# First square stage: sums of weight quadrants by VectorE additions from plain loads in place of accumulating DMAs, and the same for T3 of the FFN's down projection

## The chip, the cores and the metric

The kernel runs on one core of one Trainium2 chip. The metric is the device time of one execution in microseconds (us), lower is better. A core has TensorE (PE in the profile, with its weight loads as PEld), VectorE (DVE), ScalarE (ACT), GpSimd (POOL) and SyncE (SP, which here only issues DMAs). The engines run side by side, each works through its own queue in order, and they wait for one another by semaphores.

## The reference

One decoder block on 1024 tokens of width 1024 in float32: a mixer of two parallel branches, a cross-attention to 256 memory tokens, a SwiGLU FFN, each behind an RMSNorm and added to the residual stream, and a last RMSNorm.

```python
proj = n @ w_in                       # z, xBC, dt, q, k, v, r, a1, g_ssd, g_gla
y_ssd = ssd_mixer(z, xBC, dt_raw, ...)        # chunked scan, gated norm
y_gla = gla_mixer(q, k, v, r, a1, ...)        # gated linear attention, chunked
merged = sigmoid(g_ssd) * (y_ssd @ w_up_ssd) + sigmoid(g_gla) * (y_gla @ w_up_gla)
h = x + merged @ w_o
h = h + cross_attention(rmsnorm(h), rmsnorm(mem), w_xq, w_xkv, w_xo)
g, u = split(rmsnorm(h) @ w_ffn_in, 2)
h = h + (silu(g) * u) @ w_ffn_out
out = rmsnorm(h)
```

## The kernel before

**Arithmetic.** Activations stand transposed, features by tokens. Each float32 operand is split into a high and a low part of a faster matmul type: ACT copies the high part (`split`, L225), DVE subtracts to get the low part (the helper at L74 records all DVE and POOL operations). A product of two operands is then three matmuls, high by high, high by low and low by high, on tiles of 128 by 128 weights and 128 by 512 activations.

**Seven sub-products.** Each large matrix product is done by a Strassen scheme: both operands are cut in four quadrants, and seven sub-products on quadrants or on sums of quadrants replace eight. Their names are B11, T1, T2, B22, T3, B21, T4, in the order `LATE` where two halves of a unit or a whole square product are worked. For the weight quadrants `w(i, j)` of a square product, the left operands are:

- B11: `w(0,0)`; B21: `w(0,1)`; T4: `w(1,1)`
- T1: `w(1,0) + w(1,1)`
- T2: T1's sum `+ w(0,0)`
- B22: T2's sum `+ w(0,1)`
- T3: `w(0,0) + w(1,0)`

The right operands are quadrants of the activations `X` or sums and differences of them, formed in place by DVE.

**Square products.** `Product` (L1129) is one 1024 by 1024 product. The four of them in a row (`prods`: w_up_ssd, w_up_gla, w_o, w_xq) run in the loop at L1305, 14 steps each (7 sub-products by two halves `kk` of the contraction), 24 matmuls a step. `build` (L1153) prepares the operands of a step, `mm` (L1169) issues its matmuls and, behind the second half, the evacuation of four PSUM banks. `DEPTH = 2`: operands are built two steps ahead. `load` (L1145) fetches a weight quadrant by two plain DMAs of 512 KB on SP's queue.

**Sums by DMA.** `plus` (L230) is a DMA on GpSimd's queue that adds its source to what stands in its destination. `load("T1")` brings `w(1,0)` and lets two `plus` add `w(1,1)`. `build` issues the next `plus` as soon as a sum has been split: `w(0,0)` and `w(0,1)` onto T1's tile for T2 and B22, `w(1,0)` onto B11's tile for T3. So each tile is loaded, added to, split, added to again.

**The stage ahead.** The first product's B11 operands are prepared within the last unit of the gate projection, `group(gg[3:], B)` (L1291), whose seven steps are counted by `n`. There B11 and T1 of the weights and the four quadrants of X (from `ys_d`) are loaded and the first two `build`s stand. Raw weights of B11 and T1 take slots of the key `aux` (4 slots, also used by the gate units), B21 and T4, loaded at steps 5 and 7, take slots of `op` (14 slots). The 14 operands of the input projection (two tiles for each of seven names) occupy all of `op` until the last gate unit has used them.

**FFN-down.** The loop at L1601 runs over `todo`: 7 sub-products by 6 pieces of the contraction (two blocks of 256 rows each, the last piece one). `stream` (L1513) loads the raw tiles (`fr`: right part from `act_d`, left part from `w_ffn_out`) six pieces ahead and splits them three pieces ahead into `fs`. T1, T2 and B22 take their left parts from running sums (`rs`, made by `plus`). T3 is `w(0,0)` by a plain load and `w(1,0)` by `plus` on top. The evacuation of a sub-product (`fevac`, L1568) writes into `o`; `fpost` transposes finished quadrants on PE, two of them behind each piece of T3 and of T4.

**Order.** The framework compiles the whole program into one queue per engine: it takes instructions in order of priority (program order, shifted by `high_priority` blocks such as `ahead()`), passes over what isn't ready by its own timing model, and hands out pool slots as they come free. So SP's order is not quite the order of the source lines.

Of the kernel before, what the change touches and what calls it, by code (L numbers as in the profile page):

```python
# [16 lines left out]
P = 128  # L17
# [3 lines left out]
HALF = TOK // 2  # L21
# [6 lines left out]
KP = D_FF // 256  # L28
# [51 lines left out]
def block_kernel(ctx: ExitStack, tc: tile.TileContext, t: dict, out: bass.AP):  # L80
# [147 lines left out]
    def plus(dst, src):  # L228

        nc.gpsimd.dma_start(out=dst, in_=src, accum_op=ALU.add)  # L230
# [4 lines left out]
    class Operands:  # L235
# [14 lines left out]
        def __init__(s, hb, kh, first=None, key="op", swap=0, last_key=None, order=None):  # L250
            s.B, s.kh, s.key, s.done, s.swap = {}, kh, key, 0, swap
            s.order = order or tuple(s.PLAN)
            s.last_key = last_key or key
            s.steps = s.build(hb, kh, first or (lambda *a: None))
# [874 lines left out]
    class Product:  # L1129
# [4 lines left out]
                 "B22": ((1, 1), None), "T3": ((0, 1), (sub, (1, 1), (0, 1))), "B21": ((1, 0), None),  # L1134
                 "T4": ((1, 0), (sub, (0, 0), (1, 0)))}

        def __init__(s, W, X, c, first, last, before=lambda n, late: None):
            s.W, s.X, s.first, s.last, s.before = W, X, first, last, before
            s.tags = (acc, bank) if c == 0 else (bank, acc)
            s.raw, s.hl = {}, {}  # L1140

# [3 lines left out]
        def load(s, name, key="op"):  # L1145
            r = s.raw[name] = slot(key, (P, 2, 2, HALF), name="raw")
            for kk in range(2):
                SP.dma_start(r[:, kk], s.w(*s.RAW[name], kk))
            if name == "T1":
                for kk in range(2):  # L1150
                    plus(r[:, kk], s.w(1, 1, kk))

        def build(s, t):  # L1153
            n, kk = divmod(t, 2)
            name = LATE[n]
            of, comb = s.RIGHT[name]
            q = lambda ij: s.X.quadrant(*ij)[:, 2 * kk:2 * kk + 2]
            x = [slot("op", (P, 2, 2, HALF), F32R, name="lr") for _ in range(2)]
            raw = s.raw[{"T2": "T1", "B22": "T1", "T3": "B11"}.get(name, name)][:, kk]
            split(raw, x[0][:, 0], x[0][:, 1], either(raw))  # L1160
            more = {"B11": (1, 0), "T1": (0, 0), "T2": (0, 1)}.get(name)
            if more:
                plus(raw, s.w(*more, kk))
            if comb:
                comb[0](either(raw, 1.0), q(of), q(comb[1]), q(comb[2]))
            split(q(of), x[1][:, 0], x[1][:, 1], either(raw), name == "T2")
            s.hl[t] = x
# [113 lines left out]
    def pre_xq(n, late):  # L1281
        if n == 5 and not late:
# [1 line left out]
            s1.close(1)  # L1284
            DVE.tensor_scalar(xsc, s1.r, XSC, None, ALU.mult)

    prods = [Product(t["w_up_ssd"], x_ys, 1, copied(y_ys), last_ys, pre_ys),
             Product(t["w_up_gla"], x_yg, 0, copied(x_wo), last_yg, pre_yg),
             Product(t["w_o"], x_wo, 1, *residual(r_wo, x_xq, h1_d, s1, "norm_xattn"), pre_wo),
             Product(t["w_xq"], x_xq, 0, copied(x_o), last_xq, pre_xq)]  # L1290
    for n, _ in enumerate(group(gg[3:], B)):  # L1291
        if n == 0:
            prods[0].load("B11", "aux")
            prods[0].load("T1", "aux")
        if n < 2:
            x_ys.load(ys_d, 0, n)
        elif n < 4:
            prods[0].build(n - 2)
        elif n < 6:
            x_ys.load(ys_d, 1, 5 - n)  # L1300
    settle_all()
    sums["m"] = pool("sa2", 2, stack=st5)

# [1 line left out]
    for t_ in range(4 * 14):  # L1305
        st, n = divmod(t_, 14)
        nxt, m = divmod(t_ + DEPTH, 14)
        if nxt < 4:
            prods[nxt].build(m)
        if n in (5, 7):  # L1310
            prods[st].load("B21" if n == 5 else "T4")
        elif n in (8, 9) and st < 3:
            prods[st + 1].load("B11" if n == 8 else "T1")
        if st == 0 and 6 <= n < 10:
            x_yg.load(yg_d, *((0, 0), (0, 1), (1, 1), (1, 0))[n - 6])
        prods[st].mm(n)

    kv = {}
# [177 lines left out]
    fq = lambda u, i, j: f_o[u][:, i, half(j)]  # L1496
    LEFT = {"B11": (0, 0), "B21": (0, 1), "T3": (0, 0), "T4": (1, 1)}
    todo = [(n, k, min(2, KP - k)) for n in range(7) for k in range(0, KP, 2)]
    raws, ops, run_sums = [], [], {}

    def w_out(i, j, k, kn):
        return t["w_ffn_out"][256 * k:256 * (k + kn), half(i)].rearrange("(k j p) c -> j p k c", j=2, p=P)[j]
# [10 lines left out]
    def stream(n_raw, n_ops):  # L1513

        while len(raws) < min(n_raw, len(todo)):
            n, k, kn = todo[len(raws)]
            name = LATE[n]
            r = slot("op", (P, 2, 2, HALF), name="fr")[:, :, :kn]
            SP.dma_start(r[:, 1], act_d[(n * KP + k) * P:(n * KP + k + kn) * P, :].rearrange("(k p) s -> p k s", p=P))
            if name in LEFT:  # L1520
                SP.dma_start(r[:, 0], w_out(*LEFT[name], k, kn))
            if name == "T3":
                plus(r[:, 0], w_out(1, 0, k, kn))
            raws.append(r)
        while len(ops) < min(n_ops, len(todo)):
            n, k, kn = todo[len(ops)]
            keys = ("op", ("aux", "aux", "m", "m", "op", "op")[k // 2]) if n == 6 else ("op", "op")
            x = [slot(key, (P, 2, 2, HALF), F32R, name="fs")[:, :, :kn] for key in keys]
            r, name = raws[len(ops)], LATE[n]
            with ahead():  # L1530
                split(r[:, 0] if name in LEFT else run_sums[k], x[0][:, 0], x[0][:, 1])
                if name in ("T1", "T2"):
                    plus(run_sums[k], w_out(0, LATE.index(name) - 1, k, kn))
                split(r[:, 1], x[1][:, 0], x[1][:, 1], neg=name == "T2")
            ops.append(x)
# [132 lines left out]
```

## Time and profile before

| | |
|---|---|
| median of 3 runs | 1966.55 us (1963.18 to 1967.26) |
| the profiled execution | 1970.81 us, of which the span of the profile is 1969.1 us |
| mean granted TensorE clock | 0.983 |
| 8 accumulating DMAs of w_up_ssd, first and last issue | 812.4 and 866.5 us |
| 6 accumulating DMAs of T3 in FFN-down, first and last issue | 1837.1 and 1871.2 us |

Times in the profile count from the start of the span. In a timeline a row has the start, the time from the first start to the last end, engine, line, operation, output and inputs, and the count of instructions merged; a bracket at its end is the idle time of the engine before it and what ended it. Matmuls overlap by pipelining, so single durations are longer than the spacing of their starts. A queue (`SPq`) row is the issue of a DMA, not its transfer. A window row has the length, then the busy time and number of instructions of PE, PEld, DVE, ACT and POOL, then the granted clock, the busy share of the DMA engines and GB/s.

### The profile page before, as it was taken

To read this page: it belongs to the slowest core of one execution; us is meant where nothing else is said; L and a number is where in the kernel's file an instruction comes from. 1 tells how busy PE (TensorE), PEld (TensorE's weight loads), DVE (VectorE), ACT (ScalarE), POOL (GpSimd) and SP (SyncE) were. 2 spreads that over 40 slices of the span, in tenths; PEclk is the share of its full clock that TensorE was granted. 3 is DMA by queue.
4 is the path that set the end of the run, shared out by engine and by line. 5 is a ranking of instruction groups with operands and counts; after the bars stand their busy time and mean duration, and the time that the engine had idled before them with its cause. 6 is when DMAs were issued, how large, how long until landed. Compare 5 with 4: busy or idle time off the path is not lost.

```text
span 1969.1 us, 25777 instructions
## 1 busy us (share of the span) xinstructions
PE 1886.7 (96%) x9500; PEld 1578.4 (80%) x9500; DVE 1388.8 (71%) x2128; ACT 990.3 (50%) x1674; POOL 258.4 (13%) x235
## 2 busy tenths in 40 slices
PE   7899999999999999979989999989999999999998
PEld 6898788877788888758868887868888888888788
DVE  5866668778786665448788787797677777764474
ACT  7535556565554554354536656564333433443352
POOL 1001100164553000011110010010000000001100
PEclk9999999999999999989999999989999999999999
DMA  8532434467566563877676723622233234498962
GB/s 276 177 119 73 156 128 171 145 200 219 174 193 198 162 189 124 260 183 178 151 201 186 179 65 52 194 97 80 86 125 111 80 107 134 116 316 220 240 209 86
DMA packets 242611, 313.23 MB, mean 159 GB/s; under 512 B 14747, under 2 KB 150149, under 8 KB 242485
## 3 DMA queue, kind: packets, MB, share of 16 engines
q1 hardware_dynamic: 225588, 279.08, 42.4%
q0 software_dynamic: 16896, 32.51, 10.3%
q8 instruction: 74, 1.21, 0.3%
q14 instruction: 53, 0.43, 0.1%
HBM read 226.28 MB, written 85.26 MB: 158 GB/s over the span
## 4 chain that ended last, share of the span: by engine, by line
PE 62%; issue 15%; DMA 9%; DVE 5%; ACT 4%; POOL 3%; SPq 1%; POOLq 0%; ACTq 0%; DVEq 0%
PE acc L52 49%; PE bank L52 12%; DVE X L74 1%; PE bank L56 1%; POOL raw L230 1%; DMA csb<-cs_d 1%; DMA rs<-in_w_ffn_out_dram 1%; DVE lr L74 1%; DMA fr<-in_w_ffn_out_dram 1%; ACT lr L225 1%; DVE wlo L74 1%; DMA raw<-in_w_up_gla_dram 1%; ACT e L874 1%; POOL rs L230 1%; DMA xT_d<-xs 0%
## 5 line engine op out<-in xcount | busy, mean ns | idle before, releaser
L225 ACT ACTIVATE whi<-raw 128x512 fp32r<-128x512 f32 x224 | 140.3, 630 | 174.1 <-PE acc L52 156.2
L52 PE MATMUL acc<-lr 128*128 128x512 f32 x864 | 205.2, 395 | 16.7 <-ACT o L368 6.2
L52 PEld LDWEIGHTS acc<-lr 128*128 128x128 f32 x864 | 163.3, 190 | 53.6 <-ACT o L368 6.6
L52 PE MATMUL bank<-lr 128*128 128x512 f32 x816 | 197.2, 401 | 8.7 <-ACT lr L225 3.1
L74 DVE TENSOR_TENSOR wlo<-raw,whi 128x512 fp32r<-128x512 f32 x224 | 157.5, 706 | 66.0 <-ACT whi L225 65.9
L52 PEld LDWEIGHTS bank<-lr 128*128 128x128 f32 x816 | 157.8, 194 | 45.0 <-ACT lr L225 3.5
L225 ACT ACTIVATE whi<-sa 128x512 fp32r<-128x512 f32 x144 | 90.7, 630 | 164.5 <-PE acc L52 114.7
L74 DVE TENSOR_TENSOR o<-acc,o 128x512 f32<-128x512 f32 x144 | 99.0, 688 | 71.8 <-PE acc L52 71.5
L74 DVE TENSOR_TENSOR lr<-raw,lr 128x1024 fp32r<-128x1024 f32 x70 | 85.4, 1220 | 91.1 <-ACT lr L225 91.1
L74 DVE TENSOR_TENSOR wlo<-sa,whi 128x512 fp32r<-128x512 f32 x144 | 105.3, 732 | 50.3 <-ACT whi L225 49.2
L225 ACT ACTIVATE lr<-raw 128x1024 fp32r<-128x1024 f32 x70 | 73.9, 1055 | 111.7 <-DMA raw<-in_w_up_ssd_dram 41.4
L52 PE MATMUL acc<-fs 128*128 128x512 f32 (+1 forms) x660 | 125.3, 349 | 0.0
L52 PEld LDWEIGHTS acc<-fs 128*128 128x128 f32 x660 | 107.1, 190 | 15.6
L74 DVE TENSOR_TENSOR fs<-fr,fs 128x1024 fp32r<-128x1024 f32 (+1 forms) x60 | 66.2, 1131 | 40.0 <-ACT fs L225 40.0
L52 PE MATMUL bank<-fs 128*128 128x512 f32 x396 | 90.2, 389 | 0.0
L52 PEld LDWEIGHTS bank<-fs 128*128 128x128 f32 x396 | 74.3, 188 | 15.4
L225 ACT ACTIVATE fs<-fr 128x1024 fp32r<-128x1024 f32 (+1 forms) x60 | 57.1, 981 | 58.9 <-DMA fr<-in_w_ffn_out_dram 28.2
L230 POOL DMA_DIRECT2D rs<-in_w_ffn_out_dram x18 | 21.1, 1254 | 474.9 <-DVE wlo L74 371.0
L52 PE MATMUL acc<-T1h,whi 128*128 128x512 f32 x192 | 76.6, 399 | 3.2 <-ACT whi L225 3.2
L52 PE MATMUL acc<-B22h,wlo 128*128 128x512 f32 x192 | 75.3, 392 | 3.6 <-DVE wlo L74 3.6
L52 PE MATMUL acc<-B11h,whi 128*128 128x512 f32 x192 | 76.1, 396 | 2.5 <-ACT whi L225 2.5
L52 PE MATMUL acc<-T2h,wlo 128*128 128x512 f32 x192 | 75.4, 393 | 2.9 <-DVE wlo L74 2.9
(395 smaller groups left out, 4961.8 us busy)
## 6 DMA issues: line engine op xcount, KB each, us to landing
raw<-in_w_in_dram SPq DMA_DIRECT2D x26, 1024.0 KB, 6.1
raw<-in_w_ffn_in_dram SPq DMA_DIRECT2D x22, 1024.0 KB, 8.3
act_d<-o SPq DMA_DIRECT2D x77, 256.0 KB, 2.3
fr<-act_d SPq DMA_DIRECT2D x35, 512.0 KB, 5.2
fr<-in_w_ffn_out_dram SPq DMA_DIRECT2D x20, 512.0 KB, 5.8
raw<-in_w_xkv_dram SPq DMA_DIRECT2D x8, 1024.0 KB, 10.8
csb<-cs_d SPq DMA_DIRECT2D x16, 512.0 KB, 4.9
h_d<-ga SPq DMA_DIRECT2D x32, 256.0 KB, 2.1
```

The source lines that it names most:

```text
L52: return s.e.matmul(o, x, y, **kw)
L56: return s.e.transpose(o, x, i)
L74: return f(*a, **kw)
L225: ACT.activation(hi, src, AF.Copy)
L230: nc.gpsimd.dma_start(out=dst, in_=src, accum_op=ALU.add)
L874: ACT.activation(s.e[:, h], s.csb[:, h], AF.Relu, bias=cs[:, s.i0 + h:s.i0 + h + 1], scale=-1.0)
```

## The change

In the first square product (`plain=True`) there are no accumulating DMAs. B11, T1's `w(1,0)`, T4's `w(1,1)` and B21's `w(0,1)` are fetched by plain loads, all four within the last gate unit, between the loads of X. A new tile S in an `op` slot holds the running sum, and DVE adds into it: `w(1,0) + w(1,1)` for T1, `+ w(0,0)` for T2, `+ w(0,1)` for B22; for T3, B11's tile is added onto T1's. `build(1)` goes from step 3 to step 6 of the gate unit, `build(0)` from 2 to 4. The loads of B21 and T4 at steps 5 and 7 of the product stay for the other three products. The loads of the second product's X (`x_yg`), at steps 6, 7, 8, 9 before, come at 6, 7, 9, 10.

In FFN-down, T3's second addend `w(1,0)` is fetched by three plain loads (of four, four and three blocks) into slots of the key `m`, and DVE adds it to the raw tile ahead of the split.

```diff
+        def left(s, name, kk):
+            r = lambda x: s.raw[x][:, kk]
+            if not s.plain:
+                return r({"T2": "T1", "B22": "T1", "T3": "B11"}.get(name, name))
+            if name == "T3":
+                add(DVE, r("T1"), r("T1"), r("B11"))
+                return r("T1")
+            if name in ("T1", "T2", "B22"):
+                if "S" not in s.raw:
+                    s.raw["S"] = slot("op", (P, 2, 2, HALF), name="raw")
+                x, y = {"T1": ("T1", "T4"), "T2": ("S", "B11"), "B22": ("S", "B21")}[name]
+                add(DVE, r("S"), r(x), r(y))
+                return r("S")
+            return r(name)
...
-            raw = s.raw[{"T2": "T1", "B22": "T1", "T3": "B11"}.get(name, name)][:, kk]
+            raw = s.left(name, kk)
             split(raw, x[0][:, 0], x[0][:, 1], either(raw))
...
-            if more:
+            if more and not s.plain:
                 plus(raw, s.w(*more, kk))
...
         if n == 0:
+            x_ys.load(ys_d, 0, 0)
             prods[0].load("B11", "aux")
+        elif n == 1:
             prods[0].load("T1", "aux")
-        if n < 2:
-            x_ys.load(ys_d, 0, n)
-        elif n < 4:
-            prods[0].build(n - 2)
-        elif n < 6:
-            x_ys.load(ys_d, 1, 5 - n)
+            prods[0].load("T4")
+        elif n == 2:
+            x_ys.load(ys_d, 0, 1)
+        elif n == 3:
+            x_ys.load(ys_d, 1, 1)
+        elif n == 4:
+            prods[0].load("B21")
+            prods[0].build(0)
+        elif n == 5:
+            x_ys.load(ys_d, 1, 0)
+        else:
+            prods[0].build(1)
...
-        if n in (5, 7):
+        if n in (5, 7) and st:
             prods[st].load("B21" if n == 5 else "T4")
...
-        if st == 0 and 6 <= n < 10:
-            x_yg.load(yg_d, *((0, 0), (0, 1), (1, 1), (1, 0))[n - 6])
+        if st == 0 and n in (6, 7, 9, 10):
+            x_yg.load(yg_d, *{6: (0, 0), 7: (0, 1), 9: (1, 1), 10: (1, 0)}[n])
...
             if name == "T3":
-                plus(r[:, 0], w_out(1, 0, k, kn))
+                if k % 4 == 0:
+                    more.append(slot("m", (P, 2, 2, HALF), name="fa"))
+                    kk = min(4, KP - k)
+                    SP.dma_start(more[-1].rearrange("p a b c -> p (a b) c")[:, :kk], w_out(1, 0, k, kk))
+                other[len(raws)] = more[-1][:, k // 2 % 2, :kn]
...
+            if name == "T3":
+                add(DVE, r[:, 0], r[:, 0], other[len(ops)])
             with ahead():
                 split(r[:, 0] if name in LEFT else run_sums[k], x[0][:, 0], x[0][:, 1])
```

More of the change, by code (lines that the diff above doesn't have):

```diff
@@ L1135, in block_kernel, with __init__ @@
                  "T4": ((1, 0), (sub, (0, 0), (1, 0)))}
-        def __init__(s, W, X, c, first, last, before=lambda n, late: None):
-            s.W, s.X, s.first, s.last, s.before = W, X, first, last, before
+        def __init__(s, W, X, c, first, last, before=lambda n, late: None, plain=False):
+            s.W, s.X, s.first, s.last, s.before, s.plain = W, X, first, last, before, plain
             s.tags = (acc, bank) if c == 0 else (bank, acc)
@@ L1148, in load @@
                 SP.dma_start(r[:, kk], s.w(*s.RAW[name], kk))
-            if name == "T1":
+            if name == "T1" and not s.plain:
                 for kk in range(2):
                     plus(r[:, kk], s.w(1, 1, kk))
+        def left(s, name, kk):
[12 more added lines that the diff above has]
+            return r(name)
         def build(s, t):
@@ L1285, in pre_xq @@
             DVE.tensor_scalar(xsc, s1.r, XSC, None, ALU.mult)
-    prods = [Product(t["w_up_ssd"], x_ys, 1, copied(y_ys), last_ys, pre_ys),
+    prods = [Product(t["w_up_ssd"], x_ys, 1, copied(y_ys), last_ys, pre_ys, plain=True),
              Product(t["w_up_gla"], x_yg, 0, copied(x_wo), last_yg, pre_yg),
@@ L1498, in block_kernel @@
     todo = [(n, k, min(2, KP - k)) for n in range(7) for k in range(0, KP, 2)]
-    raws, ops, run_sums = [], [], {}
+    raws, ops, run_sums, more, other = [], [], {}, [], {}
     def w_out(i, j, k, kn):
```

## The prediction

> **What bounds the kernel now.** I read the page first (busy shares), then PE's timeline for its idle stretches, then who waited for whom inside those stretches.
>
> ```profile
> PE 1886.7 (96%) x9500; PEld 1578.4 (80%) x9500; DVE 1388.8 (71%) x2128; ACT 990.3 (50%) x1674; POOL 258.4 (13%) x235
> ```
>
> PE is busy for 1886.7 of 1969.1 us, so an edit that leaves PE's work alone can win only the 82 us in which PE stands still and what it loses at a low clock. This change touches two places of that kind. The first is the w_up_ssd product, seen in PE's timeline (start, duration, count, and in brackets the idle time before):
>
> ```profile
> 827.13 4.70 PE L52 MATMUL bank<-lr 128*128 128x512 f32 x20
> ...
> 842.82 11.01 PE L52 MATMUL acc<-lr 128*128 128x512 f32 x39 [6.20 <-ACT o L368]
> ...
> 862.49 10.79 PE L52 MATMUL bank<-lr 128*128 128x512 f32 x39 [2.31 <-ACT X L1218]
> ...
> 875.21 10.50 PE L52 MATMUL acc<-lr 128*128 128x512 f32 x45 [1.26 <-ACT X L1218]
> 885.54 11.04 PE L52 MATMUL bank<-lr 128*128 128x512 f32 x48
> ...
> 907.30 11.04 PE L52 MATMUL bank<-lr 128*128 128x512 f32 x48
> 918.18 11.04 PE L52 MATMUL acc<-lr 128*128 128x512 f32 x48
> ```
>
> One of the seven sub-products is 48 matmuls. At full pace it takes 918.18 - 907.30 = 10.88 us, or 0.2267 us a matmul. The first, B11, ends at 827.13 + 20 x 0.2267 = 831.66. The six others need 6 x 10.88 = 65.3 us and would end at 896.9, but the next product starts at 918.18. So **21.2 us** are lost here, all of it before 885.54. The windows say how (span, PE, PEld, DVE, ACT, POOL busy, granted clock, DMA share, GB/s):
>
> ```profile
> 831.80:875.20 43.40, 29.09 (x100) 21.61 (x99) 17.34 (x16) 19.18 (x27) 6.71 (x6) 0.84 0.67 146
> 840.00:846.00 6.00, 3.18 (x8) 2.50 (x9) 4.25 (x4) 3.78 (x7) 1.20 (x1) 0.50 0.64 129
> ```
>
> PE idles 43.40 - 29.09 = 14.3 us, and its 100 matmuls take 29.1 us instead of 22.7 because the granted clock is 0.84 (0.50 around the 6.20 us gap). The waits of that stretch (total, times, longest) name the cause:
>
> ```profile
> ACT lr L225 <- DMA raw<-in_w_up_ssd_dram: 40.0, 6, 15.8
> DVE lr L74 <- ACT lr L225: 36.6, 7, 10.8
> ...
> PE acc L52 <- ACT o L368: 6.2, 1, 6.2
> ```
>
> ACT's split of the weights waits for `raw`, DVE waits for ACT, and PE for both. Even the 6.20 us gap, put down to the evacuation `o`, has this cause: that evacuation stands in ACT's queue behind a split that waits for `raw`. DVE is not the limit: 17.3 us busy in 43.4. What `raw` waits for is the accumulating DMA (form with min/median/max ns, first and last start; then the time to landing):
>
> ```profile
> L230 POOL DMA_DIRECT2D raw<-in_w_up_ssd_dram x8: 1204/1212/1396, 812.4 to 866.5; - x8
> L230 POOL DMA_DIRECT2D fr<-in_w_ffn_out_dram x6: 1213/1218/1418, 1837.1 to 1871.2; - x6
> DMA to landing us min/median/max: 5.6/6.3/13.0
> ```
>
> Eight of them spread over 54 us, at 6.3 us and more each, while the sums form a chain: load, add, split, add, split. PE needs a half sub-product every 5.44 us. The chain is slower than PE.
>
> The second place is T3 of FFN-down (PE, then ACT, then DVE):
>
> ```profile
> 1824.85 30.08 PE L52 MATMUL bank<-fs 128*128 128x512 f32 x132
> 1854.77 5.60 PE L52 MATMUL acc<-fs 128*128 128x512 f32 x24
> 1864.06 1.97 PE L56 MATMUL bank<-ident,o 128*128 128x128 f32 x8 [3.69 <-DVE o L74]
> 1865.68 6.54 PE L52 MATMUL acc<-fs 128*128 128x512 f32 x24
> 1872.06 1.04 PE L56 MATMUL bank<-ident,o 128*128 128x128 f32 x8
> 1872.85 19.33 PE L52 MATMUL acc<-fs 128*128 128x512 f32 x84
> 1892.02 30.08 PE L52 MATMUL bank<-fs 128*128 128x512 f32 x132
> ...
> 1859.95 2.01 ACT L225 ACTIVATE fs<-fr 128x1024 fp32r<-128x1024 f32 x2 [4.24 <-DMA fr<-in_w_ffn_out_dram]
> ...
> 1861.04 2.36 DVE L74 TENSOR_TENSOR fs<-fr,fs 128x1024 fp32r<-128x1024 f32 x2 [3.89 <-ACT fs L225]
> 1863.32 2.48 DVE L74 TENSOR_TENSOR o<-o,bank 128x512 f32<-128x512 f32 x4
> ```
>
> B22, with the same 132 matmuls, takes 1854.77 - 1824.85 = 29.92 us. T3 takes 37.25, of which two blocks of transposes explain 2 x 0.79 = 1.6. **5.7 us** are lost: 3.69 idle, the rest slow matmuls right after it. The transposes wait for `o`, whose evacuation stands in DVE's queue behind a split that waits for ACT, which waits for the accumulating DMA into `fr`.
>
> **The change part by part.** *Removed:* 8 + 6 accumulating DMAs on POOL's queue. Their issue (1.2 us each) hides beside POOL's idle time, so nothing comes from that; the gain is the two stalls.
>
> *Moved:* the loads of T4 and B21 of the first product go ahead to the last gate unit, each two 512 KB DMAs on SP. The rows that bound their arrival (PE's last B11 matmul of that unit, two SP issues, the first split):
>
> ```profile
> 804.24 0.39 PE L52 MATMUL acc<-B11h,wlo 128*128 128x512 f32 x1
> ...
> 788.89 4.58 SPq L1124 DMA_DIRECT2D X<-ys_d  x4
> 803.73 4.19 SPq L1148 DMA_DIRECT2D raw<-in_w_up_ssd_dram  x4
> ...
> 809.74 1.06 ACT L225 ACTIVATE lr<-raw 128x1024 fp32r<-128x1024 f32 x1 [1.41 <-DMA raw<-in_w_up_ssd_dram]
> ```
>
> T4's slot is free once the unit's B11 operands are used (804.5), so SP can issue T4 right behind the four raw loads, near 808. Those landed about 6 us after issue (803.73 to 809.74), so T4 is in by about 815 and B21 a few us later. T1's first operands are needed at 831.66. Past them SP carries stores and X loads, which nobody on PE awaits at that time; X keeps its place, since SP issued it at 788.89, well before the raws, though the program has it behind them. `x_yg` for n = 8, 9 goes to 9, 10: needed a product later, cost nothing.
>
> *Added:* 8 VectorE additions of 128x1024 in the first product, 6 in T3 (the last of 128x512), and three plain loads for the second T3 addend. The price of an addition, DVE's gap ahead of T1, the window totals of first and second product, and the one sub-product of the second that lost time:
>
> ```profile
> L74 DVE TENSOR_TENSOR X<-X x72: 678/1212/1226, 814.3 to 1321.8; 128x1024 f32<-128x1024 f32 x40, 128x512 f32<-128x512 f32 x32
> ...
> 832.09 1.23 DVE L74 TENSOR_TENSOR lr<-raw,lr 128x1024 fp32r<-128x1024 f32 x1 [10.83 <-ACT lr L225]
> ...
> 831.70:918.20 86.50, 72.19 (x290) 57.21 (x290) 56.41 (x61) 42.39 (x56) 11.67 (x10) 0.92 0.72 182
> 918.20:994.60 76.40, 76.40 (x337) 62.78 (x335) 57.56 (x69) 39.33 (x53) 8.52 (x7) 1.00 0.67 162
> ...
> 950.82 11.30 PE L52 MATMUL bank<-lr 128*128 128x512 f32 x48
> 961.96 11.04 PE L52 MATMUL acc<-lr 128*128 128x512 f32 x48
> ```
>
> The eight cost 8 x 1.21 = 9.7 us of DVE. Stage after: 56.4 + 9.7 = 66.1 us of DVE in 65.3 us looks full. But the 10.8 us of DVE idle time ahead of 832 take T1's two additions and four splits (6 x 1.2 = 7.3 us), so about 59 remain for 65. The second product holds 57.6 us of DVE in 76.4 with PE at 76.40. (All other sub-products of the second product take 10.88 us; the one quoted takes 11.14.) Behind an addition on DVE stand the splits of the same step and, with priority, the evacuations; PE awaits a split only two steps (10.9 us) later, which is the cover. Without it each addition would show, 9.7 us. Bounds of what stays of the stall: nothing (all covered), or the 9.7 us, or the 6.20 us gap with its slow clock. I take 11.14 - 10.88 = 0.26 us for each of the six sub-products, 1.6 us, by the row of the neighbouring product, which is nearest: same work, same tiles, about the same DVE load.
>
> A rule bears on what a small remaining stall costs. The rows: behind the 6.20 us gap 39 matmuls take 11.0 us, and behind the 2.31 us gap 10.8, where 39 x 0.2267 is 8.8. By the Trainium skill (TensorE: Matmul & The Clock Gate, "What's actually happening") the clock falls to half only after an idle window of about 3.4 us, so gaps as short as 2.31 us would cost nothing beyond themselves. By that rule a rest of 1.6 us of short gaps is 1.6 us; by the rows (6.4 us of slow matmuls for 14.3 idle) it may be 2.3. The sum would be 25.1 by the rule and 24.4 by these rows (1942.2 us). The trace speaks against the rule, but I keep 1.6, because the 0.26 us it is built on is a loss in elapsed time and holds its slow clock already.
>
> In T3 the six additions cost 5 x 1.21 + 0.68 = 6.7 us of DVE. Bounds: nothing, or 6.7 us if each delays a split that PE awaits. The raw loads were issued early enough:
>
> ```profile
> 1842.00 0.49 SPq L1521 DMA_DIRECT2D fr<-in_w_ffn_out_dram  x1
> ```
>
> That is the fourth of T3's six; it belongs to matmuls after 1870. With landing times like the above it is in by 1848. I take nothing, and the transposes find `o` ready. The second addend needs `m` slots (two held by the output, one by a running sum until B22's splits are done): one is free, the others follow before 1843. Gain 5.7 less 0.2 for the wider DVE queue: 5.5.
>
> **Sum:** 21.2 - 1.6 + 5.5 = 25.1 us. The profiled execution took 1970.81 us (span 1969.1), 4.26 above the median 1966.55; 1970.81 - 25.1 = 1945.7 there, and **1941.5 us** for the median.
>
> **The rivals.** *A: a wait takes the stall's place.* DVE and ACT work in order: if T1's addition stands in DVE's queue before T4's load has landed, the unit's last splits and evacuation wait behind it, and the 6.20 us gap stays with the 2.2 us of slow matmuls behind it, and with the forecast's 1.6 the stage keeps 10 us. It decides when T4 lands after about 820, where the unit's last work stands on DVE. For: just this happened on ACT's queue. Against: T4's 5 us in hand. 1941.5 + 8.4 = 1950.
>
> *B: T3 isn't relieved*, because the `m` slots or SP's order bring the second addend late: 1947. For: SP issues strictly in order. Against: the slot count above.
>
> *C: given back on DVE.* The additions fill DVE to the end of the stage and their 9.7 us come out at the third product's start, where DVE is full. Against: DVE idles 18.8 us in the second product. 1941.5 + 9.7 = 1951.
>
> *D: the change doesn't do what it says*: the loads are listed in order of use, but SP's true order follows slots and readiness, and in both places plain loads land as late as the accumulating ones did. Both stalls stay: 1966.5. Against: the 6 us landing above.
>
> *E: slower.* The three extra tiles (T4, B21, S) in the 14 `op` slots leave none for operands two steps ahead. Its price is a step's chain, here at the step that ran without cover:
>
> ```profile
> 872.66 1.06 ACT L225 ACTIVATE lr<-raw 128x1024 fp32r<-128x1024 f32 x1 [4.43 <-DMA raw<-in_w_up_ssd_dram]
> ...
> 874.90 1.22 DVE L74 TENSOR_TENSOR lr<-X,lr 128x1024 fp32r<-128x1024 f32 x1
> ```
>
> From 872.66 to 876.12 are 3.5 us, with an addition 4.7. Eight steps with and four without one are 51.6 us, against 21.2 + 5.7 = 26.9 won: 1991. It decides from 15 live tiles on. My count at the fullest step (n = 9) is 13: three output quadrants, T4, B21, six operands, two raws of the next product; the sum tile is gone by then. Before, it is 13 as well.
>
> **How the numbers follow.** Forecast 0.58, A 0.15, B 0.08, C 0.05, D 0.07, E 0.07. All of both stalls gone is 1966.55 - 26.9 = 1939.7; the runs before spread 3.4 us below their median, so the range starts at 1937. It reaches to 1956, over A to C with a similar spread; D and E, 0.14, are left out. 0.2%, about what a measurement of this kernel can tell from no change, is 3.9 us: faster 0.86, same 0.07, slower 0.07.
>
> **What would show it.** PE's timeline of the w_up_ssd product as seven blocks of 48 without idle brackets and at clock 1.00, the next product starting 67 us after B11's end (86.5 before); ACT's wait for `raw` gone; T3 in 31.7 us. A bracket at T1's first matmuls naming DVE would show A; brackets naming `lr` at every step, E; an unchanged T3, B; longer gaps after the second product, C. I am wrong if T4's load lands after 820, or if a later stage turns its new head start into a wait.

## The result, and the profile after

The changed kernel takes 1945.16 us (median of 4 runs, 1942.59 to 1947.96), the kernel before 1965.85 beside it (4 runs, 1963.18 to 1967.26): a ratio of 0.9883, 95% interval [0.9864, 0.9902]. The profiled execution took 1944.69 us, its span is 1943.0. All ratios in this document leave out two executions of a later version, `third_plain`, which took 2672.89 and 9899.89 us. The following lines are the busy line of the page and PE's timeline of the w_up_ssd product (start, duration, count):

```profile
PE 1881.0 (97%) x9500; PEld 1576.5 (81%) x9500; DVE 1405.7 (72%) x2142; ACT 990.6 (51%) x1674; POOL 243.9 (13%) x221
```

```profile
831.64 11.04 PE L52 MATMUL acc<-lr 128*128 128x512 f32 x48
842.52 11.04 PE L52 MATMUL bank<-lr 128*128 128x512 f32 x48
...
886.03 11.04 PE L52 MATMUL bank<-lr 128*128 128x512 f32 x48
896.91 11.04 PE L52 MATMUL acc<-lr 128*128 128x512 f32 x48
```

B11 ends at 831.64, the next product starts at 896.91: six blocks of 48 in 65.27 us with no bracket between them. That is the ideal of the prediction (6 x 10.88), so the stall is gone to the last tenth. The window of that stretch (span; PE, PEld, DVE, ACT, POOL busy; granted clock; DMA share; GB/s), the additions on DVE (min/median/max ns, first and last start), SP's issues, and waits of the first four sub-products (total, times, longest):

```profile
831.64:896.91 65.27, 65.27 (x289) 54.07 (x288) 56.61 (x62) 35.16 (x46) 5.08 (x4) 1.00 0.52 147
```

```profile
L74 DVE TENSOR_TENSOR raw<-raw x8: 1222/1230/1233, 821.7 to 843.2; 128x1024 f32<-128x1024 f32 x8
```

```profile
788.85 4.54 SPq L1124 DMA_DIRECT2D X<-ys_d  x4
...
804.40 5.01 SPq L1148 DMA_DIRECT2D raw<-in_w_up_ssd_dram  x8
```

```profile
DVE lr L74 <- ACT lr L225: 5.9, 4, 4.1
ACT lr L225 <- PE acc L52: 5.0, 2, 4.4
...
ACT lr L225 <- DVE raw L74: 1.2, 1, 1.2
```

PE is busy for the whole 65.27 us at clock 1.00. The 40.0 us in which ACT waited for `raw` from a DMA have become 1.2 us in which it waits for an addition. SP issues all eight loads (four quadrants, two halves each) within 5 us from 804.40 on, X still ahead of them. The eight additions run between 821.7 and 844.4, on data that has long landed.

T3 of FFN-down is another matter (PE's timeline first, then DVE's, then SP's):

```profile
1832.43 5.60 PE L52 MATMUL acc<-fs 128*128 128x512 f32 x24
1838.65 1.25 PE L56 MATMUL bank<-ident,o 128*128 128x128 f32 x8 [0.62 <-DVE o L74]
...
1865.17 30.08 PE L52 MATMUL bank<-fs 128*128 128x512 f32 x132
```

```profile
1817.32 1.23 DVE L74 TENSOR_TENSOR fr<-fr,fa 128x1024 f32<-128x1024 f32 x1 [2.58 <-DMA fr<-in_w_ffn_out_dram]
...
1835.03 0.69 DVE L74 TENSOR_TENSOR fr<-fr,fa 128x512 f32<-128x512 f32 x1 [2.64 <-DMA fr<-in_w_ffn_out_dram]
1835.64 2.35 DVE L74 TENSOR_TENSOR fs<-fr,fs 128x1024 fp32r<-128x1024 f32 x2
1837.91 2.48 DVE L74 TENSOR_TENSOR o<-o,bank 128x512 f32<-128x512 f32 x4
```

```profile
1818.57 0.37 SPq L1550 DMA_DIRECT2D fa<-in_w_ffn_out_dram  x1
...
1831.67 0.42 SPq L1545 DMA_DIRECT2D fr<-in_w_ffn_out_dram  x1
```

From T3's start to T4's start it is 1865.17 - 1832.43 = 32.74 us, where 29.92 of matmuls and 1.59 of transposes make 31.51: 1.2 us are lost, against 5.7 before. The transposes still wait for the evacuation `o` at 1837.91. It stands on DVE behind the last addition, which began only when its raw tile had landed, and SP issued that tile at 1831.67. So the wait of before is still there, shorter, and it now passes through an addition. SP is also held by the change itself: the third `fa` load takes the first one's slot and could go only when the second addition (1817.32) had read that. What this costs is tested below (`t3_aux`).

From one profiled execution to the other the difference is 26.1 us: 21.2 in the first product, 4.5 in T3, about 2.1 between the second and the third product, less small losses elsewhere. The medians differ by 20.7. The experiments say which of these belong to the change.

### The profile page after: what moved, and what is told of

It reads as the page before. It is cut to its first block, busy times and chain, and to the rows that moved or that the text cites. A ratio compares the mean times of both kernels' runs of the same rounds, so it can differ in the third digit from the quotient of the medians.

```text
span 1943.0 us, 25755 instructions
## 1 busy us (share of the span) xinstructions
PE 1881.0 (97%) x9500; PEld 1576.5 (81%) x9500; DVE 1405.7 (72%) x2142; ACT 990.6 (51%) x1674; POOL 243.9 (13%) x221
## 4 chain that ended last, share of the span: by engine, by line
PE 68%; issue 10%; DMA 8%; DVE 7%; ACT 3%; POOL 2%; SPq 2%; POOLq 0%; ACTq 0%; DVEq 0%
PE acc L52 52%; PE bank L52 14%; PE bank L56 2%; DVE X L74 1%; DMA fr<-in_w_ffn_out_dram 1%; DMA raw<-in_w_in_dram 1%; DMA rs<-in_w_ffn_out_dram 1%; DVE lr L74 1%; DMA sr<-sr_d 1%; DVE wlo L74 1%; POOL rs L230 1%; POOL raw L230 1%; ACT lr L225 0%; DMA bd<-bd_d 0%; DMA raw<-in_w_o_dram 0%
## 5 line engine op out<-in xcount | busy, mean ns | idle before, releaser
L52 PE MATMUL bank<-lr 128*128 128x512 f32 x816 | 190.8, 392 | 1.4 <-ACT lr L225 1.4
```

The costliest lines, as they stand in the source:

```text
L52: return s.e.matmul(o, x, y, **kw)
```

## The experiments

Runs of one group stand beside the same runs of the kernel before; ratios are to these. All losses are read from PE's timelines as above: the first product's is the time from B11's end to the second product's start less 65.27, T3's is the time from its start to T4's less 31.51.

### The kernel before, once more

No edit.

> The kernel before once more, for a second profiled execution. The first one showed a loss of 21.2 us in the first square product and 5.7 us in T3, 26.9 together, and took 1970.8 us; the median gain of the change is only about 20.7 us. Theory L (the losses are fixed by the program): this profile shows 21 us and 5.5 us again, within 1 us, and whatever made that execution slower lies elsewhere. Rival V (the losses vary with the DMAs' timing): the first product loses 14 to 18 us here, and the execution is 4 to 6 us shorter than the first profiled one. Time against itself: ratio 1.000.

Measured: 1967.69 us (12 runs) against 1969.47 (23 runs), ratio 0.9996 [0.9982, 1.0011]. PE's timeline of its first product:

```profile
841.34 10.59 PE L52 MATMUL acc<-lr 128*128 128x512 f32 x39 [6.11 <-ACT o L368]
...
860.04 11.46 PE L52 MATMUL bank<-lr 128*128 128x512 f32 x39 [4.88 <-ACT X L1218]
```

B11 ends at 833.00, the second product starts at 915.70: 82.7 us, a loss of 17.4 where the execution that I predicted from lost 21.2. T3 loses 2.1 where that one lost 5.7. The same program, so both stalls differ by about 4 us between two executions, and the one on which the prediction was built had the larger value of both. My theory L, that the program fixes the losses, fell.

### Each part alone, and both

`first_only` has the new first product and T3 as before; `t3_only` the reverse; `both_again` is the changed kernel. The core of the first:

```diff
-                if k % 4 == 0:
-                    more.append(slot("m", (P, 2, 2, HALF), name="fa"))
...
+                plus(r[:, 0], w_out(1, 0, k, kn))
...
-            if name == "T3":
-                add(DVE, r[:, 0], r[:, 0], other[len(ops)])
```

> The first square product as changed, T3 of FFN-down with its accumulating DMAs as before. Theory (two separate stalls): first product without idle, T3 37 us as before; 16 to 21 us faster, ratio 0.989 to 0.992. Rival (the first product's gain is partly given back at the third product): the start of the third product moves by 4 us or more less than the start of the second.

> T3 of FFN-down as changed, the first square product as before. Theory: first product loses about 21 us as before; T3 takes 32.7 us instead of 37.2, 4.5 us faster, ratio 0.9977. Rival (the accumulating DMAs into T3 mattered less than the splits' order): T3 stays above 35 us, ratio 0.999 to 1.

> The changed kernel once more, beside its parts. If the parts add up, its gain is the sum of first_only and t3_only within 2 us; theory about 22 us, ratio 0.9885 to 0.990. If V holds for the changed kernel too, its profile shows a rest of stall in the first product that the first profile did not show.

| kernel | median us | ratio, 95% interval | first product loses | T3 loses |
|---|---|---|---|---|
| first_only | 1947.03 | 0.9889 [0.9869, 0.9910] | 0.0 | 0.2 |
| t3_only | 1966.78 | 0.9989 [0.9977, 1.0001] | 18.4 | 5.3 |
| both_again | 1948.50 | 0.9897 [0.9880, 0.9915] | 0.0 | 2.0 |

The first part alone has the whole gain. The second alone has none that can be told from zero: its theory, 4.5 us, fell. By the medians the two parts make 22.4 + 2.7 us and both together 21.0, a difference that the intervals don't resolve. Worse for my reason, T3 with plain loads loses 5.3 us in `t3_only`, while T3 with the accumulating DMAs loses 0.2 in `first_only`. PE's timelines of T3, `first_only` first, and DVE's of `t3_only`:

```profile
1830.76 5.61 PE L52 MATMUL acc<-fs 128*128 128x512 f32 x24
1836.21 1.04 PE L56 MATMUL bank<-ident,o 128*128 128x128 f32 x8
```

```profile
1850.19 5.60 PE L52 MATMUL acc<-fs 128*128 128x512 f32 x24
1859.24 1.97 PE L56 MATMUL bank<-ident,o 128*128 128x128 f32 x8 [3.44 <-DVE o L74]
```

```profile
1855.62 0.69 DVE L74 TENSOR_TENSOR fr<-fr,fa 128x512 f32<-128x512 f32 x1 [3.18 <-DMA fr<-in_w_ffn_out_dram]
1856.23 2.35 DVE L74 TENSOR_TENSOR fs<-fr,fs 128x1024 fp32r<-128x1024 f32 x2
1858.50 2.48 DVE L74 TENSOR_TENSOR o<-o,bank 128x512 f32<-128x512 f32 x4
```

The last addition in `t3_only` waits for a *plain* load, 5.4 us after T3 has begun. So T3's tiles can be late in either form, and I looked for the reason ahead of T3.

### Only the placement

`placed_only` has the loads of X, B11 and T1 and the first builds in their new places, but sums by accumulating DMAs (T4 and B21, which these don't need early, are loaded in the product's loop), and T3 as before:

```diff
-    prods = [Product(t["w_up_ssd"], x_ys, 1, copied(y_ys), last_ys, pre_ys, plain=True),
+    prods = [Product(t["w_up_ssd"], x_ys, 1, copied(y_ys), last_ys, pre_ys),
...
-        if n in (5, 7) and st:
+        if n in (5, 7):
```

> The loads of X, B11 and T1 and the two builds stand where the change puts them, but all sums of the first square product are made by accumulating DMAs, and T3 is as before. Theory (the chain of accumulating DMAs is the stall, the placement only makes room): the first product loses 17 to 21 us as in the kernel before, ratio 0.998 to 1.002. Rival (the placement is what counts): it loses less than 8 us.

Measured: ratio 0.9999 [0.9978, 1.0019]. PE's timeline:

```profile
843.06 10.60 PE L52 MATMUL acc<-lr 128*128 128x512 f32 x39 [6.23 <-ACT o L368]
...
862.38 10.73 PE L52 MATMUL bank<-lr 128*128 128x512 f32 x39 [2.09 <-ACT X L1234]
```

The same gaps in the same places, 18.7 us lost. The placement without the plain sums is worth nothing.

### Only the plain sums

`late_loads` is `first_only` with T4 and B21 loaded in the product's own loop (X comes first on SP in all these kernels):

```diff
+        if t_ in (0, 4):
+            prods[0].load("T4" if t_ == 0 else "B21")
```

> The first part alone with plain sums, but its loads stand where they stood in the kernel before: X first, T4 at the first and B21 at the fifth step of the product's own loop; T3 as before. Compared with the first part alone as in the change (0.9889, first product 65.28 us, loss 0). Theory: the form of the sums is what counts, and the place of the loads hardly matters as long as T4 and B21 come a few microseconds ahead of their additions: loss of the first product 0 to 3 us, ratio 0.988 to 0.991. Rival, the prediction's second mechanism: the place matters, T4 comes late, the addition for S stands at the head of VectorE's queue waiting for it and everything behind it waits too: a wait of 4 to 10 us in front of T1 or T2, first product 69 to 75 us, ratio 0.991 to 0.994.

Measured: 1949.42 us (3 runs), ratio 0.9914 [0.9886, 0.9942]. PE's and DVE's timelines, and SP's:

```profile
832.12 11.04 PE L52 MATMUL acc<-lr 128*128 128x512 f32 x48
...
897.40 11.04 PE L52 MATMUL acc<-lr 128*128 128x512 f32 x48
```

```profile
845.05 2.52 DVE L74 TENSOR_TENSOR raw<-raw 128x1024 f32<-128x1024 f32 x2 [3.51 <-DMA raw<-in_w_up_ssd_dram]
```

```profile
804.19 7.47 SPq L1148 DMA_DIRECT2D raw<-in_w_up_ssd_dram  x6
836.35 1.03 SPq L1148 DMA_DIRECT2D raw<-in_w_up_ssd_dram  x2
```

65.28 us, nothing lost. T4 is issued as early as in the change, since the order on SP isn't that of the program's text. Only B21 comes late, at 836.35, and B22's additions do wait 3.51 us for it at the head of DVE's queue; PE doesn't notice, as it needs that operand two steps later. So the rival's kind of wait is there, for B21 in place of T4, and it costs nothing. A late T4 is not tested by this run. The ratio can't be told from that of `first_only`; T3 loses 5.3 us in this profile.

### The additions doubled

`double_adds` computes each of the eight additions of the first product a second time, into a spare tile:

```diff
+                add(DVE, r("D"), r(x), r(y))
                 add(DVE, r("S"), r(x), r(y))
```

> The changed kernel with each of the eight additions of the first square product made twice, the second time into a tile that nobody reads: 9.1 to 9.7 us more of DVE in that product, 66 of 65 us if all fell into it. Theory (the additions hide two steps ahead of PE): the first product still takes 65.3 us from T1 to the next product, at most 1 us more, ratio to the kernel before as both_again, 0.988 to 0.991. Rival (DVE is full and each addition shows, there or at the start of the third product): 5 to 9 us slower than both_again, ratio 0.993 to 0.995.

Measured: ratio 0.9904 [0.9880, 0.9927]. One bracket appears:

```profile
857.18 5.74 PE L52 MATMUL acc<-lr 128*128 128x512 f32 x24 [1.32 <-DVE lr L74]
```

The product takes 899.93 - 832.96 = 66.97 us: of 9.7 us of extra DVE work 1.7 show, more than the 1 us that I allowed and far from the rival's 5 to 9. The eight additions of the change are fully covered, and by this one run that cover has about 8 us left.

### What sets T3's loss

In the 14 profiles T3's loss broadly follows one figure, the lead: how far ahead of T3's first matmul ACT starts the last large split of the running sum (`fs<-rs`, 128x1024). That sum is built by accumulating DMAs on POOL. Its splits, and those that stand behind them in the queues of ACT and DVE, free the `op` slots that T3's tiles need. ACT's rows of `before`, the changed kernel and `first_only`; they belong to T3 starts at 1854.77, 1832.43 and 1830.76:

```profile
1836.90 1.06 ACT L225 ACTIVATE fs<-rs 128x1024 fp32r<-128x1024 f32 x1 [8.05 <-DMA rs<-in_w_ffn_out_dram]
```

```profile
1810.68 1.06 ACT L225 ACTIVATE fs<-rs 128x1024 fp32r<-128x1024 f32 x1 [4.25 <-DMA rs<-in_w_ffn_out_dram]
```

```profile
1804.65 1.06 ACT L225 ACTIVATE fs<-rs 128x1024 fp32r<-128x1024 f32 x1 [4.32 <-DMA rs<-in_w_ffn_out_dram]
```

All three wait for the running sum's DMA. The leads are 17.9, 21.8 and 26.1 us, the losses 5.7, 1.2 and 0.2. SP issues T3's sixth and last raw tile accordingly: 2.8 us behind T3's start in `before` (1857.56), 0.8 ahead of it in the changed kernel, 6.7 ahead in `first_only` (and 1.5 behind in `t3_only`). That a split frees the slot is read from SP's waits, not tested by itself: in `before`, between 1800 and 1862, SP waits 41.5 us, in nine waits, for subtractions into `fs`. T3's third raw tile leaves at 1840.39, when the subtraction behind that last large split ends (1839.14 + 1.22).

In `before` there is a second way. T3's second raw tile left SP early, but POOL, which issues its accumulating DMAs one after the other, came to the one for this tile only at 1843.01. ACT waited for it until 1853.70, and SP issued the sixth raw tile when that tile's splits were done, from 1857.18 on (SP's, POOL's and ACT's rows):

```profile
1826.17 0.46 SPq L1521 DMA_DIRECT2D fr<-in_w_ffn_out_dram  x1
```

```profile
1843.01 1.22 POOL L230 DMA_DIRECT2D fr<-in_w_ffn_out_dram  x1 [4.69 <-issue]
```

```profile
1853.70 2.01 ACT L225 ACTIVATE fs<-fr 128x1024 fp32r<-128x1024 f32 x2 [8.91 <-DMA fr<-in_w_ffn_out_dram]
```

So a late running sum can make T3 late through slots and through POOL's queue. To move the lead, `rs_short` takes the kernel before and leaves one round of the chain out:

```diff
-                if name in ("T1", "T2"):
+                if name == "T1":
                     plus(run_sums[k], w_out(0, LATE.index(name) - 1, k, kn))
```

> The kernel before, with the second accumulation into FFN-down's running sum left out: B22's left operand is then the sum of T2, so this kernel leaves out one term of one product; T3 keeps its accumulating DMAs into its own tiles. Theory: T3 loses time because the chain of running-sum DMAs on POOL, one after the other at about 6.1 us, ends late, so that the last splits of the running sum free their slots late and T3's tiles are issued late. With one round of that chain gone the last large split of the running sum stands 25 us or more ahead of T3's first matmul (before: 17.9 us), T3 waits 0.3 us or less, and from T3's first matmul to the start of T4's 132 matmuls it is 31.5 to 32.1 us (before 37.3): the ratio is 0.997 to 0.999 if the run of before beside it loses 2 to 5 us there. Rival, the prediction's reason: T3's own six accumulating DMAs are late by themselves; then T3 still waits 1.5 to 4.1 us, that stretch stays at 33.6 to 37.3 us and the ratio is 1.000 within 0.001.

Measured: 1964.68 us, ratio 0.9984 [0.9969, 0.9999]; PE's timeline of T3 and ACT's last large split:

```profile
1853.73 5.61 PE L52 MATMUL acc<-fs 128*128 128x512 f32 x24
1859.17 1.04 PE L56 MATMUL bank<-ident,o 128*128 128x128 f32 x8
...
1885.43 30.08 PE L52 MATMUL bank<-fs 128*128 128x512 f32 x132
```

```profile
1824.01 1.07 ACT L225 ACTIVATE fs<-rs 128x1024 fp32r<-128x1024 f32 x1 [0.71 <-PE acc L52]
```

The split no longer waits for a DMA, its lead is 29.7 us, and T3 with its own accumulating DMAs takes 31.70 us without a bracket. So these DMAs, whose lateness I had read as the cause, are in time when the chain ahead of them is. One thing stays open: less work on POOL's queue helps T3's own accumulating DMAs there too, so `rs_short` doesn't divide the effect between slots and queue. `t3_only` has none of T3's DMAs on that queue and loses 5.3 us at a lead of 18.4, but part of that can be the third `fa` load. `third_pool_aux` (in the table) has neither and still loses 2.5 at 18.0. So the queue isn't needed for a loss; how much each way adds is not divided.

Two edits of the changed kernel bear on what is left. `t3_aux` takes the three `fa` slots from two pools in turn, so that the third load need not wait for the first tile's additions; `t3_pool` puts the additions on POOL, so that the evacuation doesn't stand behind them:

```diff
-                    more.append(slot("m", (P, 2, 2, HALF), name="fa"))
+                    more.append(slot(("m", "aux", "m")[k // 4], (P, 2, 2, HALF), name="fa"))
```

```diff
-                add(DVE, r[:, 0], r[:, 0], other[len(ops)])
+                add(POOL, r[:, 0], r[:, 0], other[len(ops)])
```

> The changed kernel, but the second of T3's three tiles of plain second addends takes a slot of aux, which a finished running sum leaves free, so that the third needn't wait in SP's queue for the first tile's additions. Theory S (SP's wait for that slot holds back the raw tiles of the last three pieces): SP issues the sixth raw tile of T3 5 us or more before T3 starts instead of at its start, the transposes wait less than 0.3 us, T3 takes 31.5 to 32 us instead of 32.7 to 36.8; 1 to 2 us faster than both_again in the trace, too little for the clock time to tell. Rival R (the raw tiles come late because the running sums free the operand slots late): unchanged, 32.7 us or more.

> The change, with T3's six additions on GpSimd in place of VectorE. Theory: what is left of T3's wait (1.2 to 2.0 us lost) is the evacuation of a bank standing behind an addition that waits for its load on VectorE, in order; with the additions on another engine the evacuation runs at once, the wait named after the evacuation falls to 0 to 0.3 us, and what remains, if anything, is a wait for the split of T3's own tile. The stretch from T3's first matmul to T4 is then 31.5 to 32.3 us. Rival: the load itself is late for the tile that PE needs, so the wait only moves from the evacuation to the weights: the stretch stays at 32.7 to 33.5 us or grows by the longer addition.

Measured: `t3_aux` 1944.07 us, 0.9881 [0.9858, 0.9904]; `t3_pool` 1940.53 us (2 runs), 0.9867 [0.9830, 0.9904]. PE's, DVE's and POOL's rows of `t3_pool`:

```profile
1827.64 5.61 PE L52 MATMUL acc<-fs 128*128 128x512 f32 x24
1833.09 1.04 PE L56 MATMUL bank<-ident,o 128*128 128x128 f32 x8
```

```profile
1816.01 8.93 DVE L74 TENSOR_TENSOR fs<-fr,fs 128x1024 fp32r<-128x1024 f32 x4 [3.38 <-ACT fs L225]
1825.80 2.73 DVE L74 TENSOR_TENSOR o<-o,bank 128x512 f32<-128x512 f32 x4 [0.87 <-PE bank L52]
```

```profile
1824.42 4.03 POOL L74 TENSOR_TENSOR fr<-fr,fa 128x1024 f32<-128x1024 f32 x2 [2.84 <-DMA fr<-in_w_ffn_out_dram]
```

The evacuation now starts 1.8 us ahead of T3's start, waiting for PE alone (in the changed kernel 5.5 us behind it), and no bracket is left, at the same lead as the changed kernel's: T3 takes 31.7 us, as the theory said. But the sixth raw tile went out earlier too, 4.6 us ahead of T3 instead of 0.8, so this one profile doesn't show which of the two removed the wait.

`t3_aux` didn't do what its theory said. The sixth raw tile was to leave 5 us or more ahead of T3 and left 1.2 ahead, and T3 takes 32.4 us, between theory and rival. From the third raw tile to the fourth SP needs 9.4 us (1814.48 to 1823.89) where the changed kernel needs 9.8: without the hold by the third `fa`, SP stands as long for an `op` slot.

All profiles in order of the lead, in us (negative: the tile was issued behind T3's start):

| kernel | T3's sum | lead of the last large split | sixth raw tile ahead of T3 | wait shown | T3 loses |
|---|---|---|---|---|---|
| placed_only | accumulating | 16.7 | -3.4 | 4.16 | 7.3 |
| before | accumulating | 17.9 | -2.8 | 3.69 | 5.7 |
| third_pool_aux | plain, two pools | 18.0 | 0.0 | 1.85 | 2.5 |
| late_loads | accumulating | 18.3 | -2.4 | 3.13 | 5.3 |
| t3_only | plain | 18.4 | -1.5 | 3.44 | 5.3 |
| before_again | accumulating | 19.8 | -0.8 | 1.50 | 2.1 |
| t3_aux | plain, two pools | 20.0 | 1.2 | 0.28 | 0.9 |
| double_adds | plain | 20.1 | -0.7 | 2.10 | 2.7 |
| both_again | plain | 21.6 | 0.4 | 1.37 | 2.0 |
| changed kernel | plain | 21.8 | 0.8 | 0.62 | 1.2 |
| t3_pool | plain, on POOL | 21.9 | 4.6 | 0 | 0.2 |
| third_plain | plain | 22.5 | 3.0 | 0 | 0.2 |
| first_only | accumulating | 26.1 | 6.7 | 0 | 0.2 |
| rs_short | accumulating | 29.7 | 8.2 | 0 | 0.2 |

The issue of the sixth raw tile orders the losses still better than the lead: from 3 us ahead on nothing is lost beyond 0.2, at 1.2 to 0 ahead it is 0.9 to 2.5, at 0.7 and 0.8 behind 2.1 to 2.7, farther behind 5.3 to 7.3. At one lead the plain form as the change has it is no better than the accumulating one (18.4 against 18.3, 20.1 against 19.8). With two pools it loses about 3 us less at a lead of 18 and 1 to 2 less at 20, with the additions on POOL 1 us less at 21.9; each of these is one profile. The medians of these versions can't be told apart.

### The third product in the same form

`third_plain` gives the w_o product plain sums too; `third_pool_aux` has its additions on POOL and T3's two pools as well:

```diff
-             Product(t["w_o"], x_wo, 1, *residual(r_wo, x_xq, h1_d, s1, "norm_xattn"), pre_wo),
+             Product(t["w_o"], x_wo, 1, *residual(r_wo, x_xq, h1_d, s1, "norm_xattn"), pre_wo, plain=True),
```

> The changed kernel with the third square product (w_o) done in the same way: T4 and B21 loaded at steps 10 and 12 of the second product, sums on DVE. Its start loses about 11 us in the changed kernel, of which T2 and B22 lose 7.9 behind accumulating DMAs that land in the order T1, T3, T2, B22. Theory: 6 to 8 us faster than both_again, ratio to the kernel before 0.985 to 0.9865. Rival (DVE is the bound at this place, since it evacuates the second product there: 20 us without a gap): the eight additions take the place of the wait, gain below 3 us.

> The change, with the sums of the third square product (w_o) by plain loads too, their seven kinds of additions on GpSimd in place of VectorE, and T3's second addends alternating between two pools of slots. Plain sums with the additions on VectorE left 128.67 us from the second product's first matmuls to the third product's T3 against 129.15 with the accumulating DMAs, with VectorE busy throughout. Theory: VectorE's work is the bound there; without the eight additions of 1.22 us that stretch falls by 4 to 8 us to 121 to 125 us, and the ratio to 0.985 to 0.987 (1936 to 1940 us). Rival: GpSimd's additions, of which 128x512 takes about 1.4 us in the profile, so some 2.8 us each for 128x1024, and which stand in one queue with its DMA issues, are themselves late: the stretch stays at 128 us or more and the waits are named after GpSimd; the ratio stays 0.988 to 0.990.

Measured: 0.9886 [0.9858, 0.9914] and 0.9922 [0.9900, 0.9943]. From the second product's start to the third's T3 it is 129.15 us in `both_again`, 128.67 in `third_plain` and 133.59 in `third_pool_aux` (11 blocks of 10.88 would be 119.7). The windows of that boundary, `third_plain` first (columns as above):

```profile
961.00:1020.00 59.00, 53.02 (x222) 41.86 (x221) 58.37 (x70) 23.53 (x27) 0.00 (x0) 0.97 0.33 107
```

```profile
961.00:1020.00 59.00, 50.20 (x201) 39.19 (x200) 57.93 (x56) 23.60 (x27) 29.59 (x8) 0.94 0.30 98
```

In `third_plain` DVE is busy for 58.37 of 59 us: the additions took the place of the wait that they removed, as the rival said. In `third_pool_aux` DVE has 14 instructions less in the same window and is just as full. DVE's groups say why (count, busy us, mean ns of one), `third_plain` first:

```profile
L74 DVE TENSOR_TENSOR lr<-raw,lr 128x1024 fp32r<-128x1024 f32 x9 | 10.9, 1215 | 0.0
...
L74 DVE TENSOR_TENSOR X<-X 128x1024 f32<-128x1024 f32 x6 | 7.2, 1215 | 0.0
```

```profile
L74 DVE TENSOR_TENSOR lr<-raw,lr 128x1024 fp32r<-128x1024 f32 x9 | 14.1, 1570 | 0.0
...
L74 DVE TENSOR_TENSOR X<-X 128x1024 f32<-128x1024 f32 x6 | 10.5, 1783 | 0.0
```

The same instructions take 29% and 47% longer while POOL adds. Over the five groups that got slower this makes 12.3 us in the window, where the eight additions had taken DVE 9.6 in `third_plain`. My theory that POOL would free DVE fell: POOL's additions cost DVE at least what they took off it. A part of the rival is seen too: ACT waits twice for a sum from POOL, 7.0 us together. The whole stretch of 133.59 us is one profile, and without any change to this product it took between 126.9 and 132.7.

## Why the prediction was right, and where it was wrong

The time lies in the range, 3.7 us above the forecast of 1941.5. Sign and mechanism of the first term held; the second term's gain did not come. The range was 19 us wide and held the time without that term too (1947), so the time alone doesn't speak for the second term.

**The first product's stall, 21.2 us.** The mechanism is shown: with the accumulating sums in their new places it stays (18.7), with plain sums it is gone, and it stays gone when B21 is issued as late as 836.35. The size was that of one execution. Five profiles with accumulating sums lose 21.2, 17.4, 18.7, 18.4 and 19.1 (`rs_short`, 833.03 to 917.43), about 19.0 in the mean.

**The 1.6 us that were to stay** are 0. The row of the neighbouring product was too dear a guide: the additions run before 844.4, where DVE had idle time, and even twice as many show only 1.7.

**T4 in by about 815** held: SP issued all eight loads between 804.40 and 809.41, and the additions from 821.66 on waited for nothing. That is also why rival A failed, and rival D for the first product. Rival E's count of slots held (no bracket names an operand). Rival C is not seen where I put it: the stretch from the second product's start to the third's T3 is 128.5 to 132.7 us in six profiles with and without the change (before 132.7 and, once more, 129.3; the changed kernel 130.6 and 129.2), with no order between them. DVE as the bound showed only when the third product got such additions.

**T3, 5.5 us: the failed step.** I put the wait for `o` down to the accumulating DMAs into `fr`, and wrote that the raw tiles "were issued early enough", from the fourth of six. The waits do name these DMAs, and one of them is a link of the wait in `before`. What failed is the step that plain loads in their place would be in time. The chain starts earlier, at the running sum, which ends late and makes T3's tiles late in either form, through the slots and through POOL's queue (`rs_short`, where it is a round shorter, loses 0.2 in T3). The fifth and sixth tiles I didn't look at. In place of 5.5 the plain form brings nothing measurable (0.9989 [0.9977, 1.0001] alone; with and without it 0.9897 and 0.9889, their intervals overlapping). Rival B, which had 0.08, is what happened. Its mechanism, SP in order, is seen, with the third `fa` held for 7.6 us; but in `t3_aux`, without that hold, SP stood as long for an `op` slot. What rival B lacked is the running sum ahead of it, which does the same without any `fa`.

**From the profiled execution to the median.** I took 25.1 off an execution that stood 4.3 us above its median, at least in part because both stalls were large in it, and carried the whole difference to the median. Without T3's 5.5, with 19.0 in place of 21.2 and nothing for the rest of 1.6, the sum is 19 us; 20.7 were measured, 21.9 for the first part alone (0.0111 x 1969). The remaining 2 to 3 us I can't place; the interval of the first part alone is about 4 us to either side.

**The clock.** I wrote that the trace speaks against the rule by which short gaps cost only themselves. T3's gaps in the table mend that. Gaps of 0.28 to 2.10 us lose 0.6 us beyond themselves, the same at every length, and 0.2 of that is lost without any gap. Behind the 2.10 us gap of `double_adds` the granted clock is 1.00 (1842.3 to 1844.0). Gaps of 3.13 to 4.16 us lose 1.9 to 3.2 beyond themselves. Behind the 3.69 us gap of `before` the clock is 0.52 (1863.9 to 1866.0), behind the 3.13 us gap of `late_loads` 0.63 (1844.8 to 1847.0). By the Trainium skill (TensorE: Matmul & The Clock Gate, "What's actually happening") the clock falls to half after an idle window of about 3.4 us. For single gaps after a long busy stretch the traces agree with that, but for some 0.4 us that short gaps cost as well, and for the place of the step, which lies between 2.10 and 3.13 us here.

The 2.31 us gap that I argued from was no single gap. It is the third in a row, behind 1.41 and 0.95 us, with nine matmuls between the first and the last. After the 6.20 us gap the clock was back at 1.00 (848 to 853), and from 858.0 to 862.5, before the 2.31 us gap was over, it was already down at 0.73.

## What to carry to other kernels

A chain of accumulating DMAs that is slower than the engine it feeds is worth replacing by plain loads and additions where the adding engine idles; look at that engine's busy time in the very stretch, because the same edit two products later, where DVE was full, brought nothing measurable. A wait that names a DMA says that it landed late, not why: follow it to its issue, and from there to what stood ahead of it in its queue and to whoever freed the tile's slot, for the last tile of the stage and not for one in the middle. And before a stall is priced from one execution, look at how far that execution stands from the median.

## What was not expected of the hardware

VectorE and GpSimd slow each other when both add tiles in SBUF: DVE's 128x1024 operations rose from 1.22 us to 1.57 and 1.78 in the mean beside POOL's additions, and in `t3_pool` four splits took 8.93 us instead of 4.7. POOL's own additions of that size took from 2.40 to 6.18 us in `third_pool_aux`. The Trainium skill (SBUF — State Buffer, "Who interferes with whom") says that a VectorE instruction with two SBUF inputs and a GpSimd instruction that reads SBUF exclude each other on a shared port; the trace agrees that both get slower. In `t3_pool` it cost nothing, since the splits were not awaited.

The accumulating DMAs of the running sum follow one another at about 6.3 us (in the changed kernel the sum's last splits start at 1798.05, 1804.42 and 1810.68), where PE takes 5.44 us for the piece that each feeds, so the chain falls behind PE by 0.9 us a piece. Why it ended 6 to 9 us earlier, against T3's start, in `first_only` than in kernels with the same code there was not settled.
